# Row factors of x traced without issue-order edges, Winograd sums paused while x is built, and a longer lead-in to the long attention

## The chip, the cores and the metric

The kernel runs on one core of one Trainium2 chip. The metric is device time in microseconds for one execution, both sequences included; smaller is better. Engines are named as in the profile: PE is TensorE's matmul, PEld its weight load, DVE is VectorE, ACT is ScalarE, POOL is GpSimd, SP is SyncE, which here issues nearly all DMAs.

## What is computed

One layer of an encoder over two sequences, a short one (1024 tokens, "s = 0") and a long one (2048 tokens, "s = 1"), each with the same 16 meta tokens ahead of it. Width 1024, all in float32.

```python
h = concat([meta, x])
xn = rmsnorm(h, g_pre)
proj = xn @ w_in + b_in                      # 6672 columns
na_q, na_k, na_v, na_z, ml_qk, ml_v, ml_z, ml_o, ml_g, mg = split(proj)
ya = (neighbourhood_attention(na_q, na_k, na_v) * silu(na_z)) @ w_a
yb = (mlstm_both_directions(conv(ml_qk), ml_v, ml_g, ml_o) * silu(ml_z)) @ w_b
ga, gb = split(sigmoid(mg))
y = (ga * ya + gb * yb) @ w_out
out = (h + rmsnorm(y, g_post))[:, 16:]
```

`rmsnorm` divides each row of h by its root mean square: `xf * rsqrt(mean(xf * xf) + EPS)`. This division by row is the "row factor" of the title.

## The kernel before

**Products in three parts.** Every float32 operand is split into a rounded high part and the rest (`xh`, `xl` for x, `whi`, `wlo` for weights), and a product is three matmuls (high·high, high·low, low·high). The splits are done by ACT (the rounding copy) and DVE (the subtraction).

**Dense and sparse.** A generator `dense` yields after every few matmuls of the projections and of the final stage; a generator `sparse` yields through the mLSTM and the attention of the short sequence, then of the long one. `run` interleaves them by estimated costs: each yield of `sparse` names a time, and dense steps are traced until they have used it up. PE executes its instructions in exactly the order traced. The instructions of the other engines and the DMA issues of SP are put in order by a list scheduler, which places each when it estimates its operands and its buffer to be ready, whatever its place in the trace. A yield of the attention (`na`) names 1.08 us for the short and 0.93 us for the long sequence.

**Held instructions.** An issue-order edge keeps an instruction behind another on the same engine. `behind()` adds such edges to all that is traced within it, to the last marked instruction of DVE, ACT and SP (`marks`: the latest evacuation of a dense product or the latest sparse step). `held()` does the same against the last traced instruction of DVE and ACT.

**Groups and jobs.** `PLAN` lists groups of projection columns for blocks of 1024 tokens: (0,0) "m", (0,0) "nv", (1,0) "mv", (1,1024) "mv", (1,1024) "ng", (1,0) "ng", (0,0) "g", and then the six blocks of the final stage. The first four are run by `group`, the next three by `sgates`, which uses Strassen-Winograd products of pairs of columns. A group is a list of jobs: feature-major jobs of four columns (`fm_half`, both halves of 512 tokens, four yields per column and half) and token-major units (`tm_unit`, 16 yields, or 18 with the meta rows). A group has three feature-major jobs; two of them come first, then the token-major units (4 for "m", 2 for "nv", 6 for "mv"), then the last feature-major job.

**Building x.** `build_half(s, t0)` makes `xh` and `xl` of 512 tokens: (0,512) during the first half of the first job; (1,0) during both halves of the last job of (0,0) "nv"; (1,512) during the first half of the first job of (1,0) "mv"; (1,1024) during both halves of that group's last job; (1,1536) during the first half of the first job of (1,1024) "mv". For the long sequence its steps are: load four blocks of 128 tokens (`tokens`, tile `xr`, L398); square and sum each on ACT (`rsum`, L355); take the reciprocal root by Newton steps on DVE (`rsqrt8`, L161 to L166); write four diagonal blocks (`rdiag`, L367 on ACT, L369 on DVE) into the buffer of the last token block; load three of the four transposed blocks of x (`xtload`, tile `xt`, L405); multiply the diagonals by a matrix of ones on PE, which puts the factor of every token on all partitions (`rrows`, L375), and copy it to `rx` (L376); load the fourth `xt`; scale (L523); split into `xh` (L530) and `xl` (L531). `xr` and `xt` and the tiles of `tprep` and `nprep` share four buffers (tag `xr`).

`spread` runs these steps from a job: 12 steps over 15 yields until the factor is applied where the build has two halves, else 22 steps over 15 yields, and all of them within `behind()`.

**Sums beside the dense work.** `beside` is called after each dense yield of `group` and `sgates`. It counts a turn (`self.turn`), issues one pending store of x (`xput`) in every third turn, and takes one step of each generator in `self.sides` when the turn is divisible by its rate: `wprep`, the Winograd sums of the weights (eight pairs of columns, 13 steps a pair; loads `pr`, sums and stores `po`, L567, L587, L591); `tprep`, those of x (loads nothing, stores `t0h` to `t3l`, L661); `nprep`, those of six more pairs of weights. `wprep` has rate 4. `tprep` has rate 4 from turn 34 for (0,0), rate 3 from turn 370 for (1,0), rate 2 with `nprep` behind it for (1,1024). What is left of `tprep` is traced at once at the start of the group's last job; what is left of `wprep` at the start of the short attention.

**The attention's start.** `na` loads the operands of its first heads (`na_prep`: `stk`, `kx`, `vr`), yields a number of times, and then goes on with the copies of the first query (`qB`, L1176) and keys. The yields are 17 for the short and 6 for the long sequence. The long attention starts while `sgates` runs; there the copy of one PSUM bank to another at L989 is part of the Winograd scheme.

Of the kernel before, what the change touches and what calls it, by code (L numbers as in the profile page):

```python
# [137 lines left out]
class K:  # L138
# [3 lines left out]
    def __init__(self, tc, ins, outs):  # L142
        self.tc, self.nc = tc, tc.nc
        self.xs = []
        self.i, self.o = ins, outs
        self.wreq, self.wraw, self.wrdy, self.wout = deque(), deque(), deque(), 0
        self.wseen, self.wkept, self.xkept = set(), {}, {}
        self.rwait = {}
        self.xput, self.turn, self.last, self.turns = deque(), 0, None, False
        self.marks = {}  # L150
        self.need = False
        self.hold, self.early = deque(), True
        self.sides, self.qd, self.TD = [], {}, {}
# [312 lines left out]
    def build_half(self, s, t0, res):  # L466

        nc, wp = self.nc, self.wp
        if (s, t0) in self.xkept:
            assert not self.xput  # L470
            yield
            yield "scaled"
            x = []
            for name, part in zip(("xh", "xl"), self.xkept[s, t0]):
                x.append(wp.tile([P, KT, HALF], F32R, name=name, bufs=2))
                for k in range(0, KT, 4):
                    nc.sync.dma_start(x[-1][:, k:k + 4, :512].bitcast(F32), part[:, k:k + 4, :])
                yield
            res.append(tuple(x))
            return  # L480
        if s == 0:
            xts = self.xnext
            self.xnext = None
            while self.rwait:
                yield "wait"
            self.early = False
            yield "scaled"
            g = self.gpre
            p = self.psum("sm", [P, 512])
            nc.tensor.matmul(p[:, :KT], self.ident, g, start=True, stop=True)  # L490
            g = self.cp.tile([P, KT], F32, name="gx")
            nc.vector.tensor_copy(g, p[:, :KT])
            x, r = self.xparts(), []
            for e in range(4):
                self.xsplit(x, xts[e], e, 0, g)
                self.wflush(2)
                yield
            res.append(tuple(x))
            yield from self.rsum(self.toks, r)
            nc.vector.tensor_copy(self.rc[:, 4:8], r[0])  # L500
            dg = self.rdiag(r[0], self.toks[0][0])

            def rows():
                self.rrows(dg, self.rr[:, 1], "sm")
                self.xp.close()
                self.wside = self.wprep()
                self.sides.append([self.wside, 4])
            self.rwait[s, t0] = rows
        else:
            bp = self.bp  # L510
            toks, r = self.tokens(s, t0, range(4), bp, 4), []
            yield
            yield from self.rsum(toks, r)
            dg = self.rdiag(r[0], toks[3][0])
            xts = [self.xtload(s, t0, e, bp, 4) for e in range(3)]
            yield
            rr = bp.tile([P, 512], F32, name="rx", tag="thT", bufs=1)
            self.rrows(dg, rr, "pj")
            xts.append(self.xtload(s, t0, 3, bp, 4))
            yield  # L520
            for k in range(KT):
                v = xts[k // 2][:, k % 2]
                nc.vector.scalar_tensor_tensor(v, v, self.gpre[:, k:k + 1], rr, op0=ALU.mult, op1=ALU.mult)  # L523
                if k % 2:
                    yield
            yield "scaled"
            x = self.xparts()
            for e in range(4):
                h = x[0][:, 2 * e:2 * e + 2, :512]
                nc.scalar.activation(h, xts[e], AF.Copy)  # L530
                nc.vector.tensor_tensor(x[1][:, 2 * e:2 * e + 2, :512], xts[e], h.bitcast(F32), op=ALU.subtract)  # L531
                yield
            res.append(tuple(x))
            self.xkeep(s, t0, x)

    def xkeep(self, s, t0, x):
# [26 lines left out]
    def wprep(self):  # L563

        nc = self.nc
        unit = {k: j for j, k in enumerate(_weight_units())}
        sub = lambda o, a, b: nc.vector.tensor_tensor(o, a, b, op=ALU.subtract)  # L567
        self.pq = ExitStack()
        pool = self.pq.enter_context(self.tc.tile_pool(name="pq", bufs=1, side="right", reuse_waits="tile"))
        for p in range(6, 14):  # L570
            raw = pool.tile([P, 2, 2, 512], F32, name="pr", bufs=1)
            for f in range(2):
                nc.sync.dma_start(raw[:, f].rearrange("p a c -> p (a c)"), self.i["wu"][unit["i", PAIRS[p][f], P], :, :D])
            for _ in range(3):
                yield
            for f, ops in ((0, ("11", "12")), (1, ("21", "22")), (1, ("s3", "s1")), (0, ("s2", "s4"))):
                if ops[0] == "s3":
                    nc.vector.tensor_tensor(raw[:, 1, 1], raw[:, 1, 0], raw[:, 1, 1], op=ALU.add)
                    sub(raw[:, 1, 0], raw[:, 0, 0], raw[:, 1, 0])
                    yield  # L580
                if ops[0] == "s2":
                    sub(raw[:, 0, 0], raw[:, 1, 1], raw[:, 0, 0])
                    sub(raw[:, 0, 1], raw[:, 0, 1], raw[:, 0, 0])
                    yield
                o = pool.tile([P, 2, 2, 512], F32R, name="po", bufs=1)
                c = slice(p > 7 and ops[0] == "21", 2)
                nc.scalar.activation(o[:, c, 0], raw[:, f, c], AF.Copy)  # L587
                sub(o[:, c, 1], raw[:, f, c], o[:, c, 0].bitcast(F32))
                for q, op in list(enumerate(ops))[c]:
                    d = self.qd[p, op] = self.dp.tile([P, D], F32, name=f"q{p}{op}")  # L590
                    nc.sync.dma_start(d[:, :], o[:, q].rearrange("p a c -> p (a c)").bitcast(F32))  # L591
                yield
                yield
# [285 lines left out]
    def spread(self, gen, chunks, until=None):  # L879

        steps = 22 if until is None else 12

        def side(last=False):
            nonlocal acc, over
            acc += steps / chunks
            while not over and (acc >= 1.0 or last):
                acc -= 1.0
                with self.behind():
                    x = next(gen, "end")
                over = x == "end" or (until is not None and x == until)  # L890
                if x == "wait":
                    break
        acc, over = 0.0, False
        return side
# [115 lines left out]
    def group(self, s, t0, meta, cols, reuse, nxt):  # L1010
# [3 lines left out]
        nb, more = None, iter(())  # L1014
        sw = (s, t0) in SW
        if sw and not reuse:
            self.tside = chain(self.tprep(s, t0, 34 if s == 0 else 370 if t0 == 0 else 0), self.nprep() if t0 else ())
            self.sides.append([self.tside, 4 if s == 0 else 2 if t0 else 3])
        for j, (kind, c) in enumerate(jobs):
            if kind == "tm":  # L1020
# [14 lines left out]
            for hf in range(2):  # L1035
                side = None
                if j == 0 and hf == 0 and not reuse:
                    side = self.spread(self.build_half(*todo[1][:2], self.xs), 15)
                elif last and nxt and nxt[0] == "f":
                    side = self.spread(self.ystart(*nxt[1:]), 15) if hf else None  # L1040
# [11 lines left out]
                for u, (col, w) in enumerate(zip(c, ws)):  # L1052
                    if hf or u:
                        with self.behind():
                            next(more, None)
                    for q, cost in enumerate(self.fm_half(col, w, self.xs[hf], *todo[hf], done=self.wdone if hf else None, tags=tags, late=late)):
                        yield cost
                        if side:
                            side()
                        if self.fout:  # L1060
                            next(self.fout, None)
                        self.beside()
                        if late is not None and u == 2 and q == 2 + hf:
                            self.rwait[todo[hf][:2]]()
                    if late is not None and u == 2:
                        for evac in late:
                            evac()
                        late = None
                        tags = iter(("tr",)) if hf else None
                        del self.rwait[todo[hf][:2]]  # L1070
# [6 lines left out]
    def na(self, s, rts):  # L1077
# [3 lines left out]
        with tc.tile_pool(name=f"na{s}{rts[0]}", bufs=1, side="right", reuse_waits="tile") as np_:  # L1081
# [11 lines left out]
            self.na_bias(rows, heads, 0)  # L1093
            for k in range(6):
                next(prep, None)
                for _ in range(2 if k else 17 - 11 * s):
                    yield A_N[s]
            cur, nxt = self.head, None
            units = [(j, cb) for j in range(n) for cb in range(4)]
# [1052 lines left out]
```

## Time and profile before

| | |
|---|---|
| runs, median (lowest to highest) | 2741.36 us (2736.14 to 2741.59), 3 runs |
| the profiled execution | 2738.11 us, of which the span of the profile is 2736.3 us |
| mean granted TensorE clock | 0.986 |
| PE, PEld, DVE, ACT, POOL busy | 97%, 85%, 71%, 53%, 1% of the span |
| DMA moved | 805.75 MB, mean 294 GB/s |

Busy shares are means over stages that have different limits. The span is that of one execution, from its first to its last instruction; times of instructions are counted from its start. In the answers, `[a <-b]` or `<-b` behind an instruction says how long its engine was idle before it and what ended that; in the list of waits the three numbers are the total in us, the count and the longest.

### The profile page before, as it was taken

Reading aid. Unit: us, or ns where it says so; the run is one execution under the profiler, and the core shown is the slowest. Engines: PE = TensorE matmul, PEld = TensorE weight load, DVE = VectorE, ACT = ScalarE, POOL = GpSimd, SP = SyncE. Lnnn points to the kernel's source line nnn. Section 1 sums busy time; section 2 is a strip of 40 time slices with the busy share of each in tenths; the row PEclk is TensorE's granted clock in tenths of the full one; section 3 lists DMA queues with packets and bytes.
Section 4 is the critical chain, followed back from the end, with each engine's and each line's share of the span. In section 5 each row is a group of like instructions: output and inputs, shape, how many; then the busy total and the mean of one; then the engine's idle time right before and its main releaser. Section 6 shows DMA issues by size and latency. Waiting matters only on the chain.

```text
span 2736.3 us, 47461 instructions
## 1 busy us (share of the span) xinstructions
PE 2652.4 (97%) x15928; PEld 2337.9 (85%) x15928; DVE 1943.8 (71%) x5266; ACT 1443.9 (53%) x3388; POOL 17.3 (1%) x100
## 2 busy tenths in 40 slices
PE   9999998899978999999999999999999999999998
PEld 7998896789967899878888878888788998989898
DVE  5665687778837978636765767757468889898954
ACT  5333555555435655436755556556365665656521
POOL 0000000000000000000000000000000000000000
PEclk9999999999989999999999999999999999999999
DMA  9899888899976999788888998899898798998965
GB/s 359 327 325 347 273 273 314 287 339 329 312 253 208 320 310 315 239 303 275 265 282 294 362 318 259 274 322 385 257 292 305 242 322 256 301 293 275 332 229 205
DMA packets 411652, 805.75 MB, mean 294 GB/s; under 512 B 52017, under 2 KB 180993, under 8 KB 409105
## 3 DMA queue, kind: packets, MB, share of 16 engines
q1 hardware_dynamic: 410288, 800.04, 87.2%
q0 software_dynamic: 1120, 2.69, 0.4%
q8 instruction: 126, 2.06, 0.3%
q14 instruction: 118, 0.96, 0.1%
HBM read 548.96 MB, written 253.60 MB: 293 GB/s over the span
## 4 chain that ended last, share of the span: by engine, by line
PE 58%; DMA 6%; DVE 4%; ACT 2%; issue 1%; SPq 0%; DVEq 0%; ACTq 0%
PE pj L962 7%; PE pj L964 7%; PE pj L963 7%; PE pj L202 5%; PE pj L203 5%; PE pj L204 5%; PE pj L1907 3%; PE pj L1908 3%; PE pj L1909 3%; PE sm L1256 2%; PE tr L1241 2%; PE pj L770 1%; PE pj L772 1%; DMA stk<-nq 1%; PE pj L771 1%
## 5 line engine op out<-in xcount | busy, mean ns | idle before, releaser
L202 PE MATMUL pj<-xh,whi 128*128 128x512 f32 (+1 forms) x896 | 346.9, 387 | 1.0 <-ACT whi L303 1.0
L203 PE MATMUL pj<-xl,whi 128*128 128x512 f32 (+1 forms) x896 | 337.0, 376 | 0.1
L204 PE MATMUL pj<-xh,wlo 128*128 128x512 f32 (+1 forms) x896 | 336.4, 375 | 0.3 <-DVE wlo L304 0.3
L770 PE MATMUL pj<-whi,xh 128*128 128x256 f32 (+1 forms) x1152 | 330.2, 287 | 0.0
L771 PE MATMUL pj<-wlo,xh 128*128 128x256 f32 (+1 forms) x1152 | 325.3, 282 | 0.0
L772 PE MATMUL pj<-whi,xl 128*128 128x256 f32 (+1 forms) x1152 | 325.2, 282 | 0.0
L1907 PE MATMUL pj<-whi,mh 128*128 128x256 f32 x768 | 219.4, 286 | 0.4 <-DMA whi<-wh 0.4
L770 PEld LDWEIGHTS pj<-whi,xh 128*128 128x128 f32 x1152 | 217.6, 189 | 0.2
L771 PEld LDWEIGHTS pj<-wlo,xh 128*128 128x128 f32 x1152 | 217.6, 189 | 0.1
L772 PEld LDWEIGHTS pj<-whi,xl 128*128 128x128 f32 x1152 | 217.5, 189 | 0.0
L1909 PE MATMUL pj<-whi,mlo 128*128 128x256 f32 x768 | 216.3, 282 | 0.0
L1908 PE MATMUL pj<-wlo,mh 128*128 128x256 f32 x768 | 216.1, 281 | 0.0
L204 PEld LDWEIGHTS pj<-xh,wlo 128*128 128x128 f32 x896 | 169.8, 189 | 32.8 <-DVE wlo L304 0.5
L202 PEld LDWEIGHTS pj<-xh,whi 128*128 128x128 f32 x896 | 170.1, 190 | 30.5 <-issue 2.1
L203 PEld LDWEIGHTS pj<-xl,whi 128*128 128x128 f32 x896 | 170.2, 190 | 27.8 <-issue 2.1
L1243 ACT ACTIVATE pts<-tr 96x384 fp32r<-96x384 f32 (+2 forms) x192 | 103.6, 539 | 103.7 <-PE tr L1241 102.9
L202 PE MATMUL pj<-yh,whi 128*128 128x512 f32 x384 | 154.5, 402 | 0.0
L203 PE MATMUL pj<-yl,whi 128*128 128x512 f32 x384 | 151.2, 394 | 0.7 <-DVE yl L1809 0.7
L204 PE MATMUL pj<-yh,wlo 128*128 128x512 f32 x384 | 151.6, 395 | 0.0
L1907 PEld LDWEIGHTS pj<-whi,mh 128*128 128x128 f32 x768 | 145.1, 189 | 1.4 <-DMA whi<-wh 0.6
L1908 PEld LDWEIGHTS pj<-wlo,mh 128*128 128x128 f32 x768 | 145.1, 189 | 0.8
L1909 PEld LDWEIGHTS pj<-whi,mlo 128*128 128x128 f32 x768 | 145.0, 189 | 0.0
(366 smaller groups left out, 6956.8 us busy)
## 6 DMA issues: line engine op xcount, KB each, us to landing
whi<-wh SPq DMA_DIRECT2D x136, 512.0 KB
wlo<-wl SPq DMA_DIRECT2D x136, 512.0 KB
whi<-q SPq DMA_DIRECT2D x62, 512.0 KB
wlo<-q SPq DMA_DIRECT2D x50, 512.0 KB
wraw<-wu SPq DMA_DIRECT2D x48, 512.0 KB
gt<-st SPq DMA_DIRECT2D x96, 256.0 KB
tg<-gt SPq DMA_DIRECT2D x96, 256.0 KB
wh<-whi SPq DMA_DIRECT2D x36, 512.0 KB
```

Of the source, the lines that this page charges most:

```text
L202: mm(out, ah, bh, start=start, stop=False)
L203: mm(out, ah, bl, start=False, stop=False)
L204: mm(out, al, bh, start=False, stop=stop)
L770: nc.tensor.matmul(o, xh, wh, start=k == 0, stop=False)
L771: nc.tensor.matmul(o, xh, wl, start=False, stop=False)
L772: nc.tensor.matmul(o, xl, wh, start=False, stop=k == KT - 1)
L962: mm(bank, w[:, 0, k], xh[:, k], start=fresh and k == 0, stop=False, skip_group_check=True)
L963: mm(bank, w[:, 0, k], xl[:, k], start=False, stop=False, skip_group_check=True)
L964: mm(bank, w[:, 1, k], xh[:, k], start=False, stop=k == 3, skip_group_check=True)
L1907: nc.tensor.matmul(o, mh[:, k, xs], wh, start=clear > 0 and k == 0, stop=False)
L1908: nc.tensor.matmul(o, mh[:, k, xs], wl, start=False, stop=False)
L1909: nc.tensor.matmul(o, ml[:, k, xs], wh, start=False, stop=clear < 2 and k == KT - 1)
```

## The change

Five edits. `self.loose` is a new flag, true except from `rrows` to the end of a build of the long sequence: while it is true, `spread` takes its steps outside `behind()`. In `group`, `beside` isn't called while a build runs (but for the short sequence's own build until `early` is unset). `wprep` has rate 3 for its first four pairs and 4 from then on. `tprep` of (1,0) starts at turn 300 in place of 370. The long attention yields 12 times in place of 6 before its first query copy (17 − 5 s in place of 17 − 11 s; the short one keeps 17).

```diff
-        self.marks = {}
+        self.marks, self.loose = {}, True
...
                 self.wside = self.wprep()
-                self.sides.append([self.wside, 4])
+                self.sides.append([self.wside, 3])
...
             rr = bp.tile([P, 512], F32, name="rx", tag="thT", bufs=1)
             self.rrows(dg, rr, "pj")
+            self.loose = False
             xts.append(self.xtload(s, t0, 3, bp, 4))
             yield
...
             res.append(tuple(x))
+            self.loose = True
             self.xkeep(s, t0, x)
...
         for p in range(6, 14):
+            if p == 10:
+                [x for x in self.sides if x[0] is self.wside][0][1] = 4
             raw = pool.tile([P, 2, 2, 512], F32, name="pr", bufs=1)
...
                 acc -= 1.0
-                with self.behind():
+                if self.loose:
                     x = next(gen, "end")
+                else:
+                    with self.behind():
+                        x = next(gen, "end")
...
-            self.tside = chain(self.tprep(s, t0, 34 if s == 0 else 370 if t0 == 0 else 0), self.nprep() if t0 else ())
+            self.tside = chain(self.tprep(s, t0, 34 if s == 0 else 300 if t0 == 0 else 0), self.nprep() if t0 else ())
...
                         if self.fout:
                             next(self.fout, None)
-                        self.beside()
+                        if side is None or s == 0 and self.early:
+                            self.beside()
...
             for k in range(6):
                 next(prep, None)
-                for _ in range(2 if k else 17 - 11 * s):
+                for _ in range(2 if k else 17 - 5 * s):
                     yield A_N[s]
```

## The prediction

> **What bounds the kernel now.** I read the page first, then the waits of TensorE (PE), then stretches around its longest waits, then the queues that feed them. The page:
>
> ```profile
> span 2736.3 us, 47461 instructions
> PE 2652.4 (97%) x15928; PEld 2337.9 (85%) x15928; DVE 1943.8 (71%) x5266; ACT 1443.9 (53%) x3388; POOL 17.3 (1%) x100
> PEclk9999999999989999999999999999999999999999
> DMA  9899888899976999788888998899898798998965
> ```
>
> PE is busy for 2652.4 of 2736.3 us, so what can be won is its 84 idle us and the time at a lower clock (one slice shows 8). The order of PE's instructions is written out by hand, so a late operand stops everything behind it. Who makes it wait (us in total, times, longest):
>
> ```profile
> PE pj L375 <- ACT xr L367: 41.9, 4, 16.4
> PE sc L1657 <- DVE q L1611: 4.4, 1, 4.4
> PE pj L962 <- ACT pj L989: 3.4, 1, 3.4
> ```
>
> Half of the idle time is one line: L375 is the product in `rrows` that spreads the four tokens-blocks' row factors over the partitions, once in each of the four builds of x of the long sequence, and it waits for the diagonals of L367. The waits and what follows them, by windows (columns: length, busy of PE, PEld, DVE, ACT, POOL, granted clock, DMA share, GB/s):
>
> ```profile
> 424.00:432.50 8.50, 0.00 (x0) 0.00 (x1) 5.07 (x22) 6.62 (x21) 0.20 (x2) 0.80 0.96 343
> 432.50:436.00 3.50, 3.50 (x6) 2.16 (x7) 0.00 (x0) 0.60 (x1) 0.00 (x0) 0.51 0.99 369
> 457.30:461.70 4.40, 0.00 (x0) 0.00 (x1) 4.28 (x8) 2.15 (x6) 0.00 (x0) 0.79 0.98 368
> 461.70:470.00 8.30, 8.27 (x32) 7.14 (x33) 4.51 (x12) 2.84 (x9) 0.10 (x1) 0.70 1.01 392
> 487.00:495.60 8.60, 0.00 (x0) 0.00 (x0) 7.40 (x39) 4.64 (x12) 0.10 (x1) 0.71 1.02 354
> 495.60:504.00 8.40, 8.34 (x26) 6.10 (x27) 7.85 (x20) 1.57 (x4) 0.00 (x0) 0.69 0.51 182
> 770.60:787.00 16.40, 0.04 (x1) 0.00 (x0) 2.45 (x14) 5.26 (x10) 0.00 (x0) 0.60 1.03 300
> 787.00:791.00 4.00, 3.92 (x7) 2.49 (x8) 1.17 (x2) 1.14 (x3) 0.00 (x0) 0.51 0.73 272
> 834.10:842.30 8.20, 0.03 (x1) 0.00 (x0) 3.60 (x18) 5.65 (x13) 0.00 (x0) 0.78 0.84 293
> 842.30:846.00 3.70, 3.64 (x8) 2.23 (x9) 0.90 (x2) 0.60 (x2) 0.00 (x0) 0.56 0.13 19
> 1969.40:1972.80 3.40, 0.00 (x1) 0.01 (x1) 1.46 (x2) 2.63 (x5) 0.00 (x0) 0.88 1.00 275
> 1972.80:1980.00 7.20, 7.20 (x20) 5.84 (x21) 1.84 (x6) 1.53 (x4) 0.00 (x0) 0.58 0.90 287
> ```
>
> The four builds, (1,0), (1,512), (1,1024) and (1,1536), stop PE at 424, 487, 770.6 and 834.1. After each, PE runs at about half its clock. Length times the missing clock: 3.5 × 0.49 = 1.7, 8.4 × 0.31 = 2.6, 4.0 × 0.49 = 2.0, 3.7 × 0.44 = 1.6, together 7.9 us. So the four stops cost 41.9 + 7.9 = 49.8 us; the one at the long attention's start costs 3.4 + 7.2 × 0.42 = 6.4; the one at 457 costs 4.4 + 8.3 × 0.30 = 6.9.
>
> [...]
>
> **Part 1: row factors made without being held.** A held instruction stands behind the last evacuation traced before it, on ScalarE, VectorE and SP. Freed, it takes its place when its operands are estimated ready. What held the chain shows in its token loads (SP's issues) and squares (ACT):
>
> ```profile
> 417.13 0.95 SPq L398 DMA_DIRECT2D xr<-x_sample  x2
> 469.55 0.86 SPq L398 DMA_DIRECT2D xr<-x_sample  x2
> 768.28 2.78 SPq L398 DMA_DIRECT2D xr<-x_sample  x4
> 824.46 4.09 SPq L398 DMA_DIRECT2D xr<-x_sample  x4
> 423.07 1.06 ACT L355 ACTIVATE xsq<-xr 128x1024 bf16<-128x1024 f32 x1 [4.00 <-DMA xr<-x_sample]
> 776.22 1.06 ACT L355 ACTIVATE xsq<-xr 128x1024 bf16<-128x1024 f32 x1 [7.63 <-DMA xr<-x_sample]
> ```
>
> From the last token issue to the end of PE's stop pass 432.5 − 418.1 = 14.4, 495.6 − 470.4 = 25.2, 787.0 − 771.1 = 15.9 and 842.3 − 828.5 = 13.8 us. Three agree on 14 to 16: the load, then squares, the Newton steps and the diagonals; I take 16. (The second had its chain held behind other work as well.) What bounds a free load is its slot among the four `xr` buffers. They are held by the split of the build before, whose last subtractions are these, and by the Winograd sums of x (`tprep`):
>
> ```profile
> 440.51 1.41 DVE L523 SCALAR_TENSOR_TENSOR xt<-xt,gpre,rx 128x512 f32<-128x512 f32 x2
> 457.96 2.35 DVE L531 TENSOR_TENSOR xl<-xt,xh 128x1024 fp32r<-128x1024 f32 x2
> 803.36 2.35 DVE L531 TENSOR_TENSOR xl<-xt,xh 128x1024 fp32r<-128x1024 f32 x2
> ```
>
> - (1,0): the sums of the short sequence's x end at turn 176, the build starts at 262 (turns are counted in the next part). The slots are free long before, so the stop at 424 goes.
> - (1,512): slots at 460.3, plus 16 is 476. PE came at 487; without the stop at 457 and its low clock it comes up to 6.9 earlier, and 1.7 of cold clock are gone too: 478.3 at worst. It goes, with 2 us to spare at worst and 11 at best.
> - (1,1536): slots at 805.7, plus 16 is 822; PE comes at 834.1 − 2.0 = 832. It goes.
>
> After L375 nothing moves against PE: `rx` is still made from that product, the steps behind it are held as before, and the fourth `xt` load still waits for the diagonals' buffer. Three `xt` loads are freed too. In the first build DVE did nothing from 432.5 to 436.0 and its first scaling came at 440.51. With those loads landed it can start with `rx`, some 4 us earlier, just ahead of the work for which PE stood at 457. That stop may go as well: 6.9 us, which I leave to the range.
>
> **Part 2: the sums rest.** `beside()` isn't called while a build runs, and only its calls count turns. A dense step of four columns has 32 turns, a token-major unit 16 (18 with the meta rows). Before, groups 0 to 2 have 166, 132 and 192 turns. After, 4, 32 and 16 + 32 fall out: 162, 100 and 144, so the builds of (1,0) and (1,512) both lie at turn 262 and that of (1,1024) at 406.
>
> - `tprep` of (1,0): 28 steps, one in three turns. Before 372 to 453, and the last job starts at 458. After 300 to 381, and it starts at 406: 25 turns ahead in place of 5. Its stores of the first and of the last slice (`t3l`, 63 turns apart) stand at
>
> ```profile
> 637.98 0.43 SPq L661 DMA_DIRECT2D t3l<-xr  x1
> 754.18 0.32 SPq L661 DMA_DIRECT2D t3l<-xr  x1
> ```
>
> 116.2 / 63 = 1.84 us a turn, so 20 turns are 37 us: the slots for (1,1024) come free about 720 and its factors can stand by 745, 25 us before PE comes at 770.6. The longest stop goes.
>
> - `wprep`: 13 turns' steps for each of eight pairs, 52 turns a pair before. After, 39 for the first four (turns 22 to 178), then 52. When (1,0)'s build starts, 4 + 84/52 = 5.6 pairs are done in place of (266 − 26)/52 = 4.6; when (1,512)'s ends, 5.6 in place of 5.5; it ends at turn 387 in place of 444 (387 and the 52 turns that fell out are 439). So one pair moves to the front, and nothing is added behind. A pair moves up to nine tiles of 512 KB, 4.7 MB. Room for it:
>
> ```profile
> 25.00:250.00 225.00, 225.00 (x1482) 205.76 (x1482) 135.81 (x206) 87.03 (x126) 0.89 (x14) 1.00 0.93 341
> 400.00:525.00 125.00, 103.33 (x495) 84.64 (x494) 96.00 (x256) 75.34 (x173) 0.71 (x6) 0.90 0.79 280
> 525.00:760.00 235.00, 232.18 (x1678) 218.66 (x1677) 189.64 (x540) 114.51 (x279) 3.08 (x13) 0.99 0.95 331
> 760.00:900.00 140.00, 114.39 (x531) 92.20 (x531) 81.74 (x190) 72.17 (x138) 0.00 (x0) 0.91 0.73 238
> ```
>
> 4.7 MB at 341 GB/s are 14 us; the DMA engines have 225 × 0.07 = 16 us free there, and VectorE 89 us. It fits barely; if that cover is gone, PE waits for weights, at most 14 us. From 400 to 525 the DMA engines work 99 us; the stretch shrinks to 125 − 21.4 = 104, and the resting sums and the earlier token loads (2 MB each) leave it. From 525 to 760 they are at 0.95, and five stores of x of 256 KB come in, 4 us of the 12 free; `tprep` is only moved within it.
>
> **Part 3: six more dense steps at the long attention's first query.** The stop at 1969 is a copy between PSUM banks standing in ACT's queue behind the copies of the first query, which wait for its load:
>
> ```profile
> 1959.19 0.49 SPq L1157 DMA_DIRECT2D stk<-nq  x1
> 1967.27 0.63 ACT L1176 ACTIVATE qB<-stk 64x512 fp32r<-64x512 f32 x1 [5.44 <-DMA stk<-nq]
> ```
>
> Six yields of 0.93 are 5.6 us of dense work traced ahead of that copy, against 5.44 us of standing. The stop goes: 6.4 us. The dense work is only brought forward; no PE work is added.
>
> **The sum.** The profiled execution took 2738.1 us, its span plus 1.8; the runs' median is 2741.4 (2736.1 to 2741.6), 3 us above, inside their own spread. 2738.1 − 49.8 − 6.4 = 2681.9. New stops are unknown: at least nothing (or −6.9 with the stop at 457), at most the 14 of the weights. From 525 to 760, where DMA and DVE are as full as they can become here, PE lost 2.8 us; twice that, 5, is my value. Forecast 2687.
>
> **Rivals.**
>
> *Only half of it.* The builds of (1,512) and (1,1536) get their slots from a build just ended; for the first the margin was 2 us at worst. If both stops stay, 11.2 + 9.8 come back: 2708. For it: DMA shares of 1.02 and 0.84 in those stops, so loads land slowly. Against it: the sums' transfers are out of these stretches.
>
> *It doesn't do what it says.* Freed instructions are placed by estimated readiness; if the estimate puts them where they stand now, only part 3 is left: 2738.1 − 6.4 + 5 = 2737. Against it: SP issued four token loads at 824.46, 19 us after their slots were free.
>
> *Slower: a freed square stands in ACT's queue.* If token loads are thought to land sooner than they do, each square stands ahead of evacuations until its block has landed. This page's waits of ACT have it already:
>
> ```profile
> ACT xsq L355 <- DMA xr<-x_sample: 16.6, 6, 7.6
> ```
>
> There are 16 such squares. The 56.2 us are used up where each costs PE 3.5 us; at 5 us the time is 2738.1 + 80 − 56 = 2762. At 7.63 us, the longest, they would cost 122. [...] Against it: ACT is busy 75 of 125 us there, and PE can run on into the other banks before an evacuation is missed.
>
> **How the numbers follow.** The forecast 0.66 (2675, with the stop at 457 gone and no new one, to 2701 with 14 more); half 0.18; no effect 0.06; slower 0.10. The range leaves out the last two and takes in the half case with its new stops up to 10 more: 2673 to 2718. Faster and slower begin at 0.2%, 5.5 us, about what runs of this kernel can tell apart: faster 0.66 + 0.18 = 0.84, same 0.06, slower 0.10.
>
> **What would show it.** Right: PE's waits no longer list L375 with more than some 5 us; token loads stand well ahead of it; `t3l` ends some 35 us ahead of the fm job; no window after 400 at a clock near 0.5; no wait for L989 at the attention's start. Wrong: PE waits for `whi` or `wlo` before 400 or between 525 and 760, or ACT's waits for token blocks grow beyond 16.6 us while PE waits for evacuations.

## The result, and the profile after

| | before | after |
|---|---|---|
| median of the runs | 2741.19 us (2736.14 to 2741.59, 4 runs) | 2710.44 us (2708.56 to 2715.00, 4 runs) |
| profiled execution, span | 2738.11 us, 2736.3 us | 2711.91 us, 2710.1 us |
| mean granted clock | 0.986 | 0.991 |

The ratio is 0.9894, 95% interval 0.9877 to 0.9912: faster, by about 30 us where 54 were forecast; 26.2 us of it show in the spans. In the changed kernel the line numbers are a little higher (L523 is L524, L531 is L532, L567 is L569, L587 is L591, L661 is L665, L1492 is L1500, L1611 is L1619, L1657 is L1665).

The page of after:

```profile
span 2710.1 us, 47468 instructions
PE 2647.9 (98%) x15928; PEld 2337.7 (86%) x15928; DVE 1942.4 (72%) x5266; ACT 1439.5 (53%) x3388; POOL 16.4 (1%) x100
PEclk9999999999999999999999999999999999999999
DMA  9888976699997899798889998899899798898975
```

PE has 62 idle us left in place of 84, and no slice of the clock shows an 8 any more. Who makes PE wait after (us in total, times, longest):

```profile
PE tr L1536 <- DVE kf L1500: 11.5, 3, 5.9
PE sc L1665 <- DVE q L1619: 10.5, 1, 10.5
...
PE pj L775 <- DMA wlo<-wl: 2.9, 1, 2.9
```

L375, which led the list with 41.9 us, is not in it. In its place stand two waits that the prediction had at nothing: `kf`, in the first states of the short mLSTM, and `q`, the stop at 457 grown from 4.4 to 10.5 us. The windows of after, at the two stops (280 to 340, and 463.8 to 484) and at the four products of L375 (columns as before: length, busy of PE, PEld, DVE, ACT, POOL, granted clock, DMA share, GB/s):

```profile
280.00:340.00 60.00, 47.63 (x293) 43.26 (x292) 37.53 (x95) 31.86 (x76) 1.91 (x10) 0.91 0.99 358
...
436.00:450.00 14.00, 13.16 (x60) 10.09 (x59) 4.59 (x11) 6.61 (x19) 0.10 (x1) 1.00 0.64 204
463.80:474.40 10.60, 0.07 (x1) 0.10 (x1) 7.79 (x13) 8.82 (x17) 0.00 (x0) 0.60 1.00 332
474.40:484.00 9.60, 9.60 (x38) 8.21 (x39) 5.59 (x16) 4.62 (x13) 0.10 (x1) 0.73 1.01 402
496.00:504.00 8.00, 8.00 (x41) 6.41 (x40) 6.22 (x25) 5.10 (x14) 0.00 (x0) 1.00 0.52 164
776.00:784.00 8.00, 8.00 (x34) 6.16 (x33) 2.62 (x4) 3.06 (x5) 0.00 (x0) 1.00 1.03 273
826.00:834.00 8.00, 8.00 (x41) 6.46 (x40) 5.17 (x12) 4.58 (x10) 0.00 (x0) 1.00 0.84 276
```

and the same 60 us of before:

```profile
280.00:340.00 60.00, 57.76 (x360) 51.71 (x359) 41.62 (x100) 34.61 (x84) 3.61 (x14) 1.00 0.86 289
```

At 440, 500, 779 and 829 us PE now runs through at a granted clock of 1.00. From 280 to 340 it does 293 matmuls where it did 360.

**Ways.** All kernels here execute the same matmuls in the same order up to the 11,122nd, so their progress can be compared by it: the time from the start of PE's n-th matmul to that of its m-th, counted in each trace. The kernels behind after are the experiments below. Behind that matmul the orders differ by a few (by the names of their tiles, in 7 of the first 11,600), and they are alike again behind the 15,268th.

| matmuls (us in before) | before | after | held | free_only | lag | chained | held_swap | swap | lag_swap | lag_sw11 |
|---|---|---|---|---|---|---|---|---|---|---|
| 0 to 1600 (to 246) | 244.5 | 245.5 | 245.6 | 245.3 | 247.0 | 246.3 | 244.7 | 245.6 | 244.3 | 244.1 |
| 1600 to 2000 (to 319) | 73.5 | 88.5 | 87.7 | 85.2 | 84.9 | 90.3 | 73.4 | 85.0 | 74.1 | 74.1 |
| 2000 to 2800 (to 449) | 129.7 | 120.3 | 128.9 | 119.3 | 126.5 | 123.1 | 131.4 | 121.5 | 124.9 | 121.9 |
| 2800 to 3200 (to 548) | 99.5 | 96.5 | 96.5 | 95.9 | 94.3 | 90.1 | 96.8 | 94.2 | 90.4 | 91.1 |
| 3200 to 4400 (to 716) | 167.4 | 171.3 | 168.5 | 167.7 | 169.6 | 172.2 | 180.3 | 177.5 | 177.5 | 176.4 |
| 4400 to 4800 (to 769) | 52.9 | 53.8 | 52.9 | 53.2 | 55.5 | 54.7 | 53.0 | 53.1 | 54.0 | 57.4 |
| 4800 to 5200 (to 881) | 112.2 | 88.4 | 108.9 | 106.4 | 88.2 | 87.1 | 108.3 | 88.0 | 88.7 | 86.7 |
| 5200 to 10800 | 1023.2 | 1020.0 | 1020.9 | 1022.1 | 1018.8 | 1021.7 | 1019.4 | 1020.2 | 1015.0 | 1018.9 |
| 10800 to 11600 | 172.4 | 165.7 | 166.5 | 172.8 | 166.7 | 165.5 | 167.1 | 166.3 | 165.4 | 167.3 |
| to the end of the span | 659.9 | 659.1 | 659.5 | 661.6 | 660.0 | 658.7 | 659.0 | 659.4 | 660.8 | 662.5 |

Column after less column before: 9.4 us are won from 2000 to 2800, 3.0 from 2800 to 3200, 23.8 from 4800 to 5200, 6.7 at the long attention's start; 15.0 are lost from 1600 to 2000 and 3.9 from 3200 to 4400.

Where the freed chain went. SP's token loads of after, the first of (1,0), of (1,512) and of (1,1024), and the last of (1,1536), with the last store of `t3l`:

```profile
298.41 0.92 SPq L398 DMA_DIRECT2D xr<-x_sample  x1
460.87 0.33 SPq L398 DMA_DIRECT2D xr<-x_sample  x1
733.96 0.55 SPq L398 DMA_DIRECT2D xr<-x_sample  x1
739.22 0.41 SPq L665 DMA_DIRECT2D t3l<-xr  x1
798.54 0.97 SPq L398 DMA_DIRECT2D xr<-x_sample  x1
```

The first of (1,0) in before:

```profile
404.47 1.39 SPq L398 DMA_DIRECT2D xr<-x_sample  x1
```

So this chain moved 106 us forward, into the middle of the first stop (the first of its three waits for `kf` ends at 297.6, ahead of it). The second stop shows in DVE's timeline of after:

```profile
450.33 1.42 DVE L524 SCALAR_TENSOR_TENSOR xt<-xt,gpre,rx 128x512 f32<-128x512 f32 x2 [5.71 <-DMA xt<-xt]
...
454.78 4.06 DVE L524 SCALAR_TENSOR_TENSOR xt<-xt,gpre,rx 128x512 f32<-128x512 f32 x6
...
473.76 0.43 DVE L1619 TENSOR_TENSOR q<-cv,q 128x256 fp32r<-128x256 f32 x1 [0.65 <-ACT q L1618]
```

The first pair that DVE scales is the one on the fourth `xt`, whose load can only follow L375 (at 439.76 in after). SP's issue of it:

```profile
443.40 0.38 SPq L405 DMA_DIRECT2D xt<-xt  x1
```

DVE stands 5.71 us for it; the six scalings on the three `xt` loaded long before come behind.

### The profile page after: what moved, and what is told of

It is laid out like the page before. It is cut to its first block, busy times and chain, and to the rows that moved or that the text cites. A ratio compares the mean times of both kernels' runs of the same rounds, so it can differ in the third digit from the quotient of the medians.

```text
span 2710.1 us, 47468 instructions
## 1 busy us (share of the span) xinstructions
PE 2647.9 (98%) x15928; PEld 2337.7 (86%) x15928; DVE 1942.4 (72%) x5266; ACT 1439.5 (53%) x3388; POOL 16.4 (1%) x100
## 4 chain that ended last, share of the span: by engine, by line
PE 72%; DMA 5%; DVE 5%; ACT 1%; issue 1%; SPq 0%; DVEq 0%; ACTq 0%
PE pj L969 7%; PE pj L971 7%; PE pj L970 7%; PE pj L202 6%; PE pj L203 6%; PE pj L204 6%; PE pj L1915 3%; PE pj L1917 3%; PE pj L1916 3%; PE pj L774 3%; PE pj L775 3%; PE pj L776 3%; PE sm L1264 3%; PE tr L1249 2%; PE sm L203 1%
## 5 line engine op out<-in xcount | busy, mean ns | idle before, releaser
L774 PE MATMUL pj<-whi,xh 128*128 128x256 f32 (+1 forms) x1152 | 331.2, 288 | 0.0
```

Source lines behind the costliest of these rows:

```text
L774: nc.tensor.matmul(o, xh, wh, start=k == 0, stop=False)
```

## The experiments

My theory: freeing wins what was forecast, and 25 us are given back by A, a stop at the short mLSTM's first states, and B, DVE standing for the fourth `xt`. Rivals: the resting sums win it, or the weight sums' rate 3 makes the new stops.

| kernel | median, us (lowest to highest, runs) | ratio to before | 95% interval |
|---|---|---|---|
| held | 2732.29 (2728.74 to 2738.75, 7) | 0.9969 | 0.9958 to 0.9980 |
| free_only | 2731.25 (2727.09 to 2733.01, 5) | 0.9961 | 0.9949 to 0.9974 |
| lag | 2714.55 (2704.92 to 2714.88, 4) | 0.9893 | 0.9876 to 0.9911 |
| chained | 2709.46 (2702.02 to 2712.23, 4) | 0.9874 | 0.9856 to 0.9892 |
| held_swap | 2731.90 (2729.48 to 2739.55, 10) | 0.9986 | 0.9970 to 1.0001 |
| swap | 2710.92 (2706.67 to 2718.03, 6) | 0.9903 | 0.9880 to 0.9927 |
| lag_swap | 2698.16 (2697.17 to 2705.87, 6) | 0.9865 | 0.9840 to 0.9890 |
| lag_swap_chained | 2703.23 (2699.74 to 2705.10, 6) | 0.9873 | 0.9851 to 0.9894 |
| after_again | 2712.58 (2709.31 to 2717.76, 6) | 0.9907 | 0.9891 to 0.9923 |
| lag_swap_again | 2705.94 (2699.79 to 2708.79, 5) | 0.9875 | 0.9859 to 0.9892 |
| lag_sw11 | 2698.32 (2696.00 to 2703.15, 4) | 0.9853 | 0.9837 to 0.9870 |
| lag_sw11_tp310 | 2704.10 (2698.54 to 2705.19, 4) | 0.9868 | 0.9851 to 0.9885 |

The first four, the next four and the last four ran on one chip each.

**held.** In `spread`:

```diff
-                if self.loose:
-                    x = next(gen, "end")
-                else:
-                    with self.behind():
-                        x = next(gen, "end")
+                with self.behind():
+                    x = next(gen, "end")
```

> The change without its first part: every step of a build is held again, while the sums still rest, tprep starts at turn 300 and the long attention has its twelve yields. Theory (freeing carries the gain, and some 25 us of it are given back at two new stops, one at 295 to 333 us where the freed factors of (1,0) stand among the short mLSTM's first states, one at 464 us where DVE stands before the scaling of the fourth xt): the waits at L375 come back with 25 to 42 us, the new stop at 295 to 333 goes, and the time is 2725 to 2738 us. Rival (the resting sums carry the gain, since the builds then run undisturbed): L375 stays below 15 us and the time is 2708 to 2718 us.

Measured 2732.29 us, with these waits, this window, and these two copies of ACT's timeline:

```profile
PE pj L375 <- ACT xr L367: 35.0, 4, 12.0
PE tr L1533 <- DVE kf L1497: 7.5, 3, 3.3
```

```profile
280.00:340.00 60.00, 50.60 (x300) 45.83 (x299) 36.24 (x85) 28.34 (x69) 3.18 (x12) 0.89 0.88 301
```

```profile
287.87 1.06 ACT L591 ACTIVATE po<-pr 128x1024 fp32r<-128x1024 f32 x1 [1.22 <-DMA q<-po]
...
307.27 1.06 ACT L591 ACTIVATE po<-pr 128x1024 fp32r<-128x1024 f32 x1 [3.96 <-DMA q9s<-po]
```

The resting sums don't carry the gain: L375 still waits 35 us. But half of my theory fell too: stop A is there with nothing freed (87.7 us from 1600 to 2000). At rate 3 the next sum's rounding copy comes before the store of the last one has left `po`, which has one buffer; ACT stands 1.22 us in front of the first copy shown and 3.96 us in front of the second, with the mLSTM's copies behind. The two stands are 5.2 us and the stretch loses 14.2. The first wait for `kf` ends at 297.7 us, ahead of the longer stand, so the stands are not shown to be the whole of it; the copies' own work in the queues of ACT and DVE may be the rest.

**free_only.** The kernel before, with `self.loose` alone (its three assignments, and the branch in `spread`).

> The kernel before with the first part alone: row factors of the long sequence's builds are not held; sums, rates and yields as before. Theory (the new stops come from freeing itself): PE's waits for kf and q in 290 to 335 and 455 to 475 us are there as in the changed kernel, 18 us or more together; three of the four waits at L375 go, the one of (1,1024) stays in part because its buffers are still late, and the copy at the long attention's start stays; 2720 to 2733 us. Rival (the new stops come from the weight sums' faster rate and earlier loads): both stops are at their old 2 and 4 us, and the time is 2703 to 2713 us.

Measured 2731.25 us. PE's waits:

```profile
PE pj L375 <- ACT xr L367: 18.3, 1, 18.3
PE tr L1533 <- DVE kf L1497: 10.1, 2, 5.2
...
PE pj L967 <- ACT pj L994: 4.1, 1, 4.1
```

```profile
280.00:340.00 60.00, 49.93 (x306) 45.39 (x306) 35.80 (x97) 31.69 (x80) 2.93 (x15) 0.91 0.82 277
```

Three of the four L375 stops go with freeing alone. The fourth, of (1,1024), stays whole, since its buffers come no earlier; the earlier `tprep` is what frees it (started ten turns later, in lag_sw11_tp310 below, it leaves a wait of 6.0 us there). The stop at the attention's start stays as well, and is gone in held, which has the twelve yields: 172.8 against 166.5 us from 10800 to 11600. The wait for `q` is 5.5 us (with `kf` 15.6, less than the 18 expected): DVE came to the fourth `xt` at 442.48 and did not stand, so B needs both halves of the change. Stop A is there, now with rate 4, from the freed chain. DVE of free_only, and the first `kf` of before:

```profile
289.08 0.17 DVE L358 TENSOR_SCALAR ss<-ss 128x4 f32<-128x4 f32 x1 [2.77 <-ACT xsq L355]
...
298.34 0.42 DVE L1497 SCALAR_TENSOR_TENSOR kf<-th,cv 128x256 f32<-128x256 f32 x1
```

```profile
292.01 0.42 DVE L1492 SCALAR_TENSOR_TENSOR kf<-th,cv 128x256 f32<-128x256 f32 x1
```

DVE stands 2.77 us for squares, and the first `kf` comes 6.3 us later. held and free_only win 8.5 and 9.6 us by themselves, the two together 30: stop A is paid by either and only once, and the longest L375 stop needs both halves.

**lag.** A middle way between held and free: a freed step stays behind the marks as they stood one job earlier.

```diff
+            self.lag.append(dict(self.marks))      # at the start of each job; two are kept
...
-                if self.loose:
-                    x = next(gen, "end")
-                else:
-                    with self.behind():
-                        x = next(gen, "end")
+                with self.behind(self.lag[0] if self.loose else None):
+                    x = next(gen, "end")
```

> The changed kernel, but a freed step is held behind the latest marks as they stood when the job before the current one began, in place of not at all: the factors of (1,0) can't be placed before the last token-major unit of the group, some 30 to 50 us ahead of their use instead of 110. Theory (the freed squares and token loads of (1,0) stand in the queues of the short mLSTM's first states): the waits for kf at 295 to 333 us fall from 9 us to 3 or less with their low clock, L375 stays gone, and the time falls by 8 to 13 us, to 2697 to 2703. Rival (the weight sums at rate 3 fill ACT and DVE there): the stop stays at 7 us or more and the time within 3 us of the changed kernel, 2707 to 2713.

Measured 2714.55 us: 1.5 us above the rival's range. The way from 1600 to 2000 improves by 3.6 us only, with the `kf` waits at 7.7, as held had led to expect (rate 3 stays), and from 2000 to 2800 6.2 us are lost. One row of its window, of ACT's timeline, and of PE's waits:

```profile
280.00:340.00 60.00, 51.53 (x311) 46.53 (x312) 38.86 (x92) 30.15 (x72) 2.68 (x12) 0.91 0.91 317
```

```profile
421.99 1.06 ACT L355 ACTIVATE xsq<-xr 128x1024 bf16<-128x1024 f32 x1 [4.22 <-DMA xr<-x_sample]
```

```profile
PE sm L202 <- ACT kth L1537: 3.6, 1, 3.6
```

Here ACT stood 4.22 us before a square, to 421.99, and PE stood 3.6 us, to 425.75, for a copy that came later in ACT's queue.

**chained.** In `build_half`, each scaling is kept behind the one traced before it.

```diff
+                with ExitStack() as st:
+                    if k:
+                        st.enter_context(self.tc.issue_after(self.scaled))
                     nc.vector.scalar_tensor_tensor(v, v, self.gpre[:, k:k + 1], rr, op0=ALU.mult, op1=ALU.mult)
+                self.scaled = ...     # this instruction
```

> The changed kernel, with each scaling step of a build kept behind the scaling step traced before it, so that the pair on the fourth xt comes last in DVE's queue and not first. Theory (DVE's stand of 5.7 us before that pair makes PE wait for q at 464 us): that wait falls from 10.5 to 5 us or less, and the time falls by 5 to 9 us, to 2701 to 2706. Rival (the squares of (1,512) and the piled-up evacuations in ACT's queue make it): the wait stays at 8 us or more, and the time at 2708 to 2712.

Measured 2709.46 us. DVE's scaling and the wait:

```profile
452.41 5.38 DVE L527 SCALAR_TENSOR_TENSOR xt<-xt,gpre,rx 128x512 f32<-128x512 f32 x8
```

```profile
PE sc L1669 <- DVE q L1623: 3.7, 1, 3.7
```

The stand is gone and the stop falls from 10.5 to 3.7 us; the stretch from 2800 to 3200 falls by 6.4 us: this stand made B grow. What is left is near the 4.4 of before (in lag, where DVE did not stand either, it was 6.7, so the stand is not all of it). The time doesn't show it (it lies in the rival's 2708 to 2712): in the profiled execution 1600 to 2800 are 4.6 us longer, and the intervals of the two ratios overlap.

**held_swap and swap.** The weight sums' rates exchanged: 4 for the first four pairs, 3 for the rest; held_swap with all steps held, swap with them free.

```diff
-                self.sides.append([self.wside, 3])
+                self.sides.append([self.wside, 4])
...
-                [x for x in self.sides if x[0] is self.wside][0][1] = 4
+                [x for x in self.sides if x[0] is self.wside][0][1] = 3
```

> The change without its first part, as in the earlier run with all steps held, and with the weight sums' rates exchanged: one step in four turns for the first four pairs, one in three for the rest. PE's way from its matmul 1600 to its matmul 2000 (the short mLSTM's first states, 246 to 335 us) took 73.5 us before, 87.7 with everything held and rate 3, 85.2 with freeing alone. Theory A1 (at rate 3 a sum's rounding copy stands in ACT's queue for the store of the sum before it, and this alone stops PE there): 73 to 77 us. Theory A2 (the shift of the turns by the resting sums does it, whatever the rate): 84 us or more. The whole time stays within 2722 to 2735 us, since L375 waits as before.

> The changed kernel with the weight sums' rates exchanged: four turns a step for the first four pairs, three for the rest. Theory A1 with the freed chain as a second, separate cause: the way from matmul 1600 to 2000 stays at 83 to 87 us, since the four squares and the token loads of (1,0) still stand there; 2705 to 2711 us. If rate 3 were the only cause it would fall to 73 to 77 and the time to 2695 to 2700. If neither, it stays at 88.

held_swap, its window and its copy at that place:

```profile
280.00:340.00 60.00, 58.12 (x359) 51.74 (x359) 41.67 (x100) 34.31 (x84) 2.85 (x14) 1.00 0.86 290
```

```profile
300.48 1.05 ACT L591 ACTIVATE po<-pr 128x1024 fp32r<-128x1024 f32 x1
```

swap, its DVE, and its wait:

```profile
445.02 1.42 DVE L524 SCALAR_TENSOR_TENSOR xt<-xt,gpre,rx 128x512 f32<-128x512 f32 x2 [2.46 <-DMA xt<-xt]
```

```profile
PE sc L1665 <- DVE q L1619: 7.3, 1, 7.3
```

Held and at rate 4, the way from 1600 to 2000 is 73.4 us, as in before; free and at rate 4 it is 85.0. So rate 3 and the early chain each make stop A alone, and the shift of the turns does not. That is A1's outcome; its mechanism, the stand for the store, is shown only as far as held showed it. swap also gives B a second size: DVE's stand is 3.25 us shorter than in the changed kernel (2.46 for 5.71), and the stop is 3.25 us shorter (7.29 for 10.54). The price of the exchange is on 3200 to 4400, 6 to 12 us, where the faster sums now lie; in swap PE waits 9.4 us for weights there.

**lag_swap, lag_swap_chained.** lag with the exchanged rates; then with the chained scaling too.

> The changed kernel with both: freed steps held behind the marks of the job before, and the exchanged rates. Theory A1 with two separate causes: the way from matmul 1600 to 2000 falls to 73 to 77 us, and the time to 2697 to 2705 us (12 us won there, up to 6 lost again where the chain of (1,0) now stands, at 420 us, and some at 525 to 715 us where the sums' loads move to). Theory A2 (the shifted turns): the stretch stays at 84 or more and the time at 2708 to 2716.

> As the run before, with the scaling of the fourth xt kept last in DVE's queue too. Theory (both stops have their causes named): 2690 to 2700 us, with the way from matmul 1600 to 2000 at 73 to 77 us and that from 2800 to 3200 at 88 to 92 (99.5 before, 96.5 in the changed kernel). If what is won at one place is lost at the next, as with the lagged marks alone: 2706 to 2713.

The window of lag_swap:

```profile
280.00:340.00 60.00, 57.17 (x356) 51.08 (x356) 41.41 (x100) 34.18 (x83) 3.32 (x14) 1.00 0.86 287
```

With both causes away stop A is gone: 74.1 us, and 2698.16 us in time. Chaining adds nothing (2703.23): in lag_swap the fourth `xt` stands last in DVE's queue already, and DVE scales from 436.4 to 442.3 without a stand; from 2800 to 3200 both need 90 to 91 us.

**The last four.** The changed kernel and lag_swap once more; lag_sw11 changes the rate from 4 to 3 at the sixth pair (`p == 11`) in place of the fifth; lag_sw11_tp310 also starts `tprep` of (1,0) at turn 310.

> The changed kernel itself once more, beside the other three on one chip: 2706 to 2713 us, with PE's way from matmul 1600 to 2000 at 86 to 90 us, from 2800 to 3200 at 95 to 98 and from 3600 to 4400 (about 615 to 725 us) at 103 to 106, as in its first profile, if these stops belong to the kernel; ways nearer the 73, 99 and 99 of before would say that they were chance.

> The kernel with lagged marks and exchanged rates once more. If its gain over the changed kernel belongs to it: 8 to 14 us less than that one on this chip, 2696 to 2703 us, and the way from matmul 1600 to 2000 again at 73 to 76 us. If it was chance: within 4 us of the changed kernel.

> Lagged marks, and the weight sums at four turns a step for five pairs and at three for the last three. It tests what the way from matmul 3600 to 4400 pays, 110 us with the exchanged rates, 104 in the changed kernel, 99 before. Theory C (the sums of weights and of x move more there than the DMA engines have room for, so that PE waits for weights): fewer steps at rate 3 end 13 turns later with less load ahead of 700 us, the way is 104 to 108 us, and the time 2 to 5 us below the kernel with exchanged rates. Rival (tprep's start at turn 300 alone fills that stretch): 110 us again and no difference.

> As the run before, with tprep of (1,0) starting at turn 310 in place of 300. Theory C: the way from matmul 3600 to 4400 falls by 2 to 4 us more, but the buffers for (1,1024) come free 18 us later, at 757 us for the last, and its factors miss PE by up to 6 us at L375: within 4 us of the run before. If the sums of x weren't what fills that stretch, only the later factors would show: 3 to 8 us slower than the run before.

Stop A is there again in after_again (88.2 us) and not in lag_swap_again (74.2); the latter is 6.6 us faster, a little less than expected. From 3600 to 4400 the four take 100.5, 113.4, 108.9 and 102.2 us. after_again itself was below its expected ways there and from 2800 to 3200 (94.3), so such ways vary by 2 to 4 us from one profile to the next. Later sums of x shorten the way by 6.7 us, as theory C says and 3 us more than it expected. For fewer steps at rate 3 that isn't shown: 108.9 is 4.5 below lag_swap_again, but only 1.6 below the first profile of lag_swap (110.5). What lag_sw11 and lag_sw11_tp310 wait for most:

```profile
PE pj L775 <- DMA wlo<-wl: 9.5, 2, 6.4
```

```profile
PE pj L375 <- ACT xr L367: 6.0, 1, 6.0
```

The later `tprep` trades this wait, at 620 to 730 us, for 6.0 us at L375, the price expected, and the time is 5.8 us above lag_sw11, not within 4. **lag_sw11 beats both kernels**: 2698.3 against 2712.6 and 2738.8 us on one chip, and its interval (0.9837 to 0.9870) lies below that of the changed kernel (0.9891 to 0.9923). That it beats lag_swap isn't shown: it is 7.6 us below lag_swap_again, more than the 2 to 5 expected, but their intervals overlap, and lag_swap had 2698.16 us in its first runs.

## Why the prediction was right, and where it was not

The sign held, and the mechanism where it won: the stops at L375 and the one at the attention's start went. The size was too large: the time is 23 us above the forecast. It lies 9 us above 2701, the forecast's own upper end, and inside the range only since that was widened to 2718 for the rival "only half", which put the time at 2708. That rival didn't come about, so that the range held, and that its number is near, is luck.

- *The four stops and their low clock, 49.8 us.* L375 is gone from the waits, and PE runs at clock 1.00 at all four. Won there: 9.4 us of 10.2 at the first and 23.8 of 28.2 at the last two; at the second 3.0 of 11.2, since B grew in the same stretch. held and free_only show that it was freeing, with the earlier `tprep` for the third stop.
- *The attention's start, 6.4 us.* 6.7 by the ways (7.5 from 10800 to the 15,300th matmul, where the orders are alike again); only kernels with twelve yields have it. Right. A stop near the 11,400th matmul, 2.7 us in before and 2.5 in after, was not part of it and stays.
- *Part 1, "After L375 nothing moves against PE", and DVE's first scaling 4 us earlier.* This step failed. I took the three freed `xt` loads for what DVE waits for, and didn't look at which scaling stands first in its queue. It is that on the fourth `xt`. In before the piled-up work behind the stop at 424 hid that load (issued at 434.60 us, the scaling at 440.51 without a stand); with the stop gone DVE came to it early and stood 5.71 us. The stop that "may go as well" grew from 4.4 to 10.5 us; without the stand, in chained, it was 3.7.
- *Part 1, (1,0): "The slots are free long before, so the stop at 424 goes."* True of the stop, but it left unasked where a chain goes that nothing holds: 106 us forward, among the first states of the short mLSTM.
- *Part 2, the faster weight sums: "at most 14 us", as a wait for weights.* Ahead of stop A their transfers cost at most the 1.0 us of the first way. What stopped PE, with nothing freed, was the rate, as held against held_swap shows, and in held a copy stood 3.96 us in ACT's queue for the store of the sum before it; the prediction counted the free time of the DMA engines and of DVE and not the order of ACT's queue. Its rows of room also leave out 250 to 400 us: the fourth pair, the last at rate 3, has its last copy at 306.1 in after, and A lies there.
- *New stops, 5 us.* This is the mis-sized term of the sum. From 1600 to 2000 alone 15.0 us were lost, from 3200 to 4400 3.9 (with the wait for `wlo` that was named as a sign, 2.9 us; in after_again the loss is 0.2), and B took 8.2 from the second L375 stop (6.0 in after_again). The ends that I gave it (nothing to 14 us) were drawn from DMA room alone. Twice 2.8 is 5.6 and not 5, and 2701 has the 14 on top of the 5, where the sum has them in its place (2696).
- *`tprep` 37 us earlier, slots about 720.* The last `t3l` store came 15.0 us earlier (739.22 for 754.18), the loads from 733.96 on; PE came at 778.8. Counted back from PE's product, the store stood 39.6 us ahead in place of 16.4, 23 us won of the 37; where the rest went is open. The conclusion held on its margin, not on its number.
- *Rival "slower: a freed square stands in ACT's queue".* Such stands are there, and in after mostly off PE's path:

```profile
ACT xsq L355 <- DMA xr<-x_sample: 22.2, 8, 11.5
```

The total grew from 16.6 to 22.2 us, past the sign that I named, and the longest, 11.5 us at 758, cost PE nothing that shows. In lag PE stood 3.6 us behind one of 4.22. In stop A the freed chain does cost, but by its own work: in free_only DVE stood 2.77 us for ACT's squares, and the three of them at 285.5 to 289.0 us did not stand for a load.
- *Rivals "only half" and "no effect".* Token loads at 460.87 and 798.54 and no wait at L375: neither came about.

## What to carry to other kernels

An instruction that is set free doesn't move to where it is wanted but to the first place where its operands are thought ready (here 106 us forward, 404.47 to 298.41); give it a lower bound (here, the marks of one job earlier) as well as freedom, and look at what it will stand beside. When a stop is removed, read the queues of the engines behind it in order: the next instruction in line may be the one whose operand the stop had covered (here the scaling of the fourth `xt`, for which DVE stood 5.71 us). ACT's idle share was no room for work that itself waits: in held ACT was busy for 28.34 of the 60 us from 280 to 340, and there a copy into a single buffer, at the faster rate, stood 3.96 us for that buffer's last store, with a copy of `kth` next behind it (PE's waits for `kth` are 2.1 us in all).

## What the runs showed of the hardware

Two idle times of PE of the same length had different prices. Windows of after: the first stop of A and what follows it, then the third stop and what follows it.

```profile
294.80:297.60 2.80, 0.02 (x1) 0.02 (x1) 2.73 (x10) 1.42 (x6) 0.00 (x0) 1.00 0.87 298
297.60:302.00 4.40, 4.40 (x19) 4.00 (x20) 3.29 (x6) 2.78 (x5) 0.00 (x0) 0.63 0.64 179
...
331.20:334.00 2.80, 0.00 (x1) 0.01 (x2) 1.59 (x6) 1.74 (x7) 0.00 (x0) 1.00 1.03 374
334.00:340.00 6.00, 6.00 (x47) 5.79 (x48) 3.99 (x11) 3.52 (x11) 0.56 (x3) 1.00 0.93 298
```

Both stops are 2.8 us long. After the first PE ran at 0.63 for 4.4 us, a loss, estimated as length times missing clock, of 4.4 × 0.37 = 1.6 us; after the second it ran at 1.00 for the 6.0 us shown. So a stop's price here is its length and, in the rows shown, nothing (the one at 331.2 in after) to 3.0 us more (the one at 1969.4 in before, 7.2 × 0.42). What sets such stops apart isn't shown: no run here was made to test it.
